# Wider rows of the token tile and wider weight-part buffers: the distance between the two operands of TensorE takes all multiples of 64 bytes

## The chip, the cores and the metric

One core of a Trainium2 chip runs the whole kernel. The metric is the device time of one execution in microseconds (us). TensorE (PE) multiplies, VectorE (DVE) and ScalarE (ACT) prepare operands and take results out of PSUM, GpSimd (POOL) fills a few tiles, and SyncE (SP) issues the weight transfers.

## What is computed

One layer of a diffusion backbone on 256 latent tokens and 256 context tokens, width D = 2048, all in float32:

```python
hx = modulate(rms_norm(x, norm1_g), sh1, sc1)          # the context tokens likewise
q, zf, zb, v, g, sb, sc, sh, ga, gb = split(hx @ w_in) # context: only zf, zb, v
o = hgrn2(q, zf, zb, v)                                # two directions, 8 heads, chunked scan
y_a = norm(o) * a_norm_g * silu(g)
y_b = sb * short_conv(sc * sh)
x = x + g1 * ((sigmoid(ga) * (y_a @ w_pa) + sigmoid(gb) * (y_b @ w_pb)) @ w_o)
a, b = split(modulate(rms_norm(x, norm2_g), sh2, sc2) @ w_up)
x = x + g2 * ((silu(dwconv3x3(a)) * b) @ w_down)
out = rms_norm(x, final_g)
```

## The kernel before, in words

**Three products for one.** Every operand of the large products is kept in two parts of type float32r, a high part and a low part (what is left of the float32 value when the high part is taken off). A product of tokens and weights is then made of three matmuls: high by high, low weights by high tokens, and high weights by low tokens.

**The tiles that TensorE reads.** `H` (line 175) holds the tokens: 128 partitions, 16 rows `k` (one for each 128 of D), and in each row four stretches of 256 elements: the latent tokens' low and high part (`hx = H[:, :, 0:2, :]`, line 176) and the context's high and low part. One row is 4 x 256 x 4 bytes = 4096 bytes. A piece of weights (128 x 2048 elements, 1 MB) comes by one SP transfer into one of four `raw` buffers (`wload`, line 70). `wsplit` (line 97) makes of each half a high part with ACT (line 118, buffer `w_hi`, five of 4096 bytes) and a low part with DVE (line 119). The low part goes to a `w_lo` buffer (five of 4096 bytes, on the right side of the memory behind the small unused tile `edge`), or, once the context's tokens are no longer needed, into the context's half of two rows of `H` (`context_parts`, `lo_ring`).

**Two shapes of matmul.** `proj` (line 399) makes 256 columns of a projection: for eight rows `k` and two halves `n` of 128 columns, a *wide* matmul (high weights loaded, `src[:, k]` moving: 512 elements, low and high tokens side by side), and then a *narrow* one (low weights loaded, `src[:, k, 1, :]` moving: 256 elements). Sixteen wide and sixteen narrow ones alternate, `wide_next` lets groups of one shape join up to 32. `token_product` (line 804) works for `w_o` and `w_down` the other way round: parts of tokens are loaded (from `mg`, or from `hx` by `y_part`), and 512 columns of `w_hi` or of a low part move; the output is named `to`. `values` (`vacc`) does the same for v, and `mm3` (line 139) with `proj_xc` and the first stage (`acx`, `zacc`) takes latent and context tokens together.

Each matmul comes with a load of its 128 x 128 weights into the array, and the load for the next matmul runs while the present one streams its moving operand. So at any time TensorE reads two places of the memory: the present matmul's moving operand and the next one's weights. I call the *distance* of such a pair the address where those weights begin, less the address where the moving operand begins, in remainder by 512 bytes.

**Addresses before.** In the built program `H` begins at byte 76288 of each partition, the `w_hi` buffers at 55808 and every 4096 after, `y_a` at 182784, `mg` at 150016. All of these, all row and buffer steps, and all slices that the products take (512, 1024 or 2048 bytes long) are multiples of 512. The `w_lo` buffers begin at 208832, which is 448 above a multiple of 512. So every pair of the products named above has the distance 0, but for those with a `w_lo` buffer: 448 where it is loaded, 64 where it moves.

**The rest that the change touches.** `cst` (line 164, `silu(c)` and `silu(c_ctx)` in 32 columns) is the weights operand of the first stage's products, and column 0 is also the scalar of line 691, where DVE sums the rows of `w_mod` for later segments. `pb` (line 162) holds the columns of `b_mod`. `squares` (line 856) writes a square that nobody reads, for the sum that comes with it. The order of the instructions on the engines is fixed when the program is built, in part by hand (`manual_schedule`, `issue_after`).

Of the kernel before, what the change touches and what calls it, by code (L numbers as in the profile page):

```python
# [9 lines left out]
F32 = mybir.dt.float32  # L10
F32R = mybir.dt.float32r
U8 = mybir.dt.uint8
AF = mybir.ActivationFunctionType
ALU = mybir.AluOpType
PSUM = bass.MemoryType.PSUM

P = 128
T = 256
D = 2048
KD = D // P  # L20
# [5 lines left out]
HB = 64  # L26
EPS = 1e-6
SPLIT = 2.0 ** 63


def strided(ap, offset, dims):
# [5 lines left out]
def hybrid_layer_kernel(ctx: ExitStack, tc: tile.TileContext, I, out, dbg=None):  # L37
    nc = tc.nc
# [3 lines left out]
    ctx_d = I["ctx"][0]  # L42
# [5 lines left out]
    cp = ctx.enter_context(tc.tile_pool(name="cp", bufs=1))  # L48
    rawp = ctx.enter_context(tc.tile_pool(name="rawp", bufs=4))
    hip = ctx.enter_context(tc.tile_pool(name="hip", bufs=5))  # L50
    hp = ctx.enter_context(tc.tile_pool(name="hp", bufs=1))
# [3 lines left out]
    lop = lop_cm.__enter__()  # L55
# [14 lines left out]
    def wload(parts):  # L70
        raw = rawp.tile([P, 2048], F32, name="raw", tag="raw")
        off = 0
        for src, shape in parts:
            n = 1
            for s in shape:
                n *= s
            dst = raw[:, off:off + n]
            if len(shape) == 2:
                dst = dst.rearrange("p (a b) -> p a b", a=shape[0])
            loads[0] = nc.sync.dma_start(dst, src)  # L80
            off += n
        return raw
# [4 lines left out]
    def lo_half():  # L87
        lo_ring.append(lo_ring.pop(0))
        return lo_ring[-1]

    def context_parts(*which):
        return [H[:, 2 * i:2 * i + 2, 2:4, :].rearrange("p a b t -> p a (b t)") for i in which]

# [3 lines left out]
    def wsplit(parts, widths=(1024, 1024), raw=None):  # L97


        if raw is None:  # L100
            raw = wload(parts)
        for i, n in enumerate(widths):
            half = raw[:, 1024 * i:1024 * i + n]
            hi = hip.tile([P, 1024], F32R, name="w_hi", tag="w_hi")[:, :n]
            if lo_ring:
                two = lambda ap: ap.rearrange("p (a n) -> p a n", a=2)
                lo = lo_half()
                operands = {"out": lo, "in0": two(half), "in1": two(hi.bitcast(F32))}
                cut = lambda a, b, lo=lo: lo[:, a // 512, a % 512:a % 512 + b - a]
            else:  # L110
                lo = lop.tile([P, 1024], F32R, name="w_lo", tag="w_lo")[:, :n]
                operands = {"out": lo, "in0": half, "in1": hi.bitcast(F32)}
                cut = lambda a, b, lo=lo: lo[:, a:b]
            with ExitStack() as behind:
                after, sub = behind_of.pop(0) if behind_of else ((), nc.vector)
                for ins in after:
                    behind.enter_context(tc.issue_after(ins.ins))
                nc.scalar.activation(hi, half, AF.Copy)  # L118
                sub.tensor_tensor(op=ALU.subtract, **operands)  # L119
            yield lambda p, a, b, hi=hi, cut=cut: cut(a, b) if p else hi[:, a:b]  # L120

    def wviews(parts, kt):

        n = 2048 // kt
        for i, part in enumerate(wsplit(parts)):
            for k in range(kt // 2):
                yield i * (kt // 2) + k, part(0, k * n, k * n + n), part(1, k * n, k * n + n)
# [8 lines left out]
    def mm(o, lhsT, rhs, start, stop):  # L136
        return nc.tensor.matmul(o, lhsT, rhs, start=start, stop=stop, skip_group_check=True)  # L137

    def mm3(o, wl, wh, k, start, stop):


        mm(o, wh, H[:, k, 1:3, :], start, False)
        mm(o, wl, H[:, k, 1:3, :], False, False)
        mm(o, wh, H[:, k, 0:4:3, :], False, stop)

# [13 lines left out]
    masks = cp.tile([P, 6, HB], U8)  # L159

    pa = cp.tile([P, 121], F32)
    pb = cp.tile([P, 96], F32)
    pf = cp.tile([P, 440], F32)
    cst = cp.tile([P, KD, 32], F32)
    lb = cp.tile([P, 16], F32)
    oml = cp.tile([P, 16], F32)
    bm = cp.tile([P, 2, 16], F32)
# [4 lines left out]

    H = hp.tile([P, KD, 4, T], F32R)
    hx = H[:, :, 0:2, :]


    first = ExitStack()
    sp = first.enter_context(tc.tile_pool(name="sp", bufs=1))  # L180
# [9 lines left out]
    for t in range(2):  # L190
        xt = xtp.tile([P, D], F32, name="xt", tag="xt")
# [5 lines left out]
    for t in range(2):  # L197
        parts = []
        for j in range(2):
            xt = lop.tile([P, 1024], F32, name="ct", tag="w_lo")  # L200
            nc.sync.dma_start(xt[:], ctx_d[t * P:t * P + P, 1024 * j:1024 * j + 1024])
            parts.append(xt[:])
        xts.append(parts)
    at = 0
    for src in (
# [6 lines left out]
        n = src.shape[0]  # L212
# [4 lines left out]
    def to_cols(dst, src, n):  # L217
        pt = psH.tile([P, 512], F32, name="pt", tag="psh")
        nc.tensor.transpose(pt[:, :n], src, ident[:n, :n])
        nc.vector.tensor_copy(dst, pt[:, :n])  # L220

    nc.vector.memset(cst[:], 0.0)
    to_cols(pa[:, 0:32], rows_c[:], 32)
    sg_c = sp.tile([P, 32], F32)
    nc.scalar.activation(sg_c[:], pa[:, 0:32], AF.Sigmoid)
    for i in range(2):
        nc.vector.tensor_tensor(out=cst[:, :, i], in0=pa[:, 16 * i:16 * i + 16], in1=sg_c[:, 16 * i:16 * i + 16], op=ALU.mult)

    ssq = sp.tile([P, 2, 4], F32)
    rstd = sp.tile([P, 4], F32)  # L230
    junk = H[:, 0].rearrange("p b c -> p (b c)")
    for i in range(2):
# [133 lines left out]
    with tc.manual_schedule(engines={nc.tensor.engine, nc.vector.engine, nc.scalar.engine}):  # L366
# [4 lines left out]
        for b, (k0, nk) in enumerate(blocks):  # L371
# [4 lines left out]
            if b + 1 < len(blocks):  # L376
                n = {0: (2, 8), 6: (5, 4), 7: (0, 3)}.get(b, (4, 6))
# [113 lines left out]
    def hgrn(g, ft, q):  # L491
# [10 lines left out]
        gc = gp.tile([P, 2, 2, T], F32, name="gc", tag="gc")  # L502
        nc.vector.tensor_scalar(out=X[:, 0:2], in0=ft[:, :, 0], scalar1=1.0 / SPLIT, scalar2=None, op0=ALU.max)
        nc.vector.tensor_scalar(out=gc[:], in0=ft[:, :, 1], scalar1=1.0 / SPLIT, scalar2=None, op0=ALU.max)
        nc.vector.tensor_scalar(out=ft[:], in0=ft[:], scalar1=SPLIT, scalar2=1.0, op0=ALU.mult, op1=ALU.min)
        nc.scalar.activation(X[:, 0:2], X[:, 0:2], AF.Ln)
# [174 lines left out]
    def mod_steps():  # L681
        for seg in (4, 3, 2, 5):
            acc = map_.tile([P, D], F32, name="macc", tag="macc")
            with ExitStack() as behind:
                if seg == 5:
                    behind.enter_context(tc.issue_after(h2_lo[KD // 2 - 1].ins))
                nc.gpsimd.memset(acc[:], 0.0)
            nc.gpsimd.dma_start(acc[0:1, :], b_mod[0:1, seg * D:seg * D + D])
            for k in range(KD):
                raw = wload([(w_mod[k * P:k * P + P, seg * D:seg * D + D], (2048,))])  # L690
                nc.vector.scalar_tensor_tensor(out=acc[:], in0=raw[:], scalar=cst[:, k, 0:1], in1=acc[:], op0=ALU.mult, op1=ALU.add)  # L691
                if k < KD - 1:
                    yield
            if seg in (3, 4):
                col = sh2 if seg == 3 else g2c
                for k4 in range(KD // 4):
                    pc = psH.tile([P, 4, P], F32, name="pc", tag="psh")
                    for k in range(4):
                        at = (4 * k4 + k) * P
                        nc.tensor.transpose(pc[:, k, :], acc[:, at:at + P], ident[:])  # L700
                    nc.vector.tensor_reduce(out=col[:, 4 * k4:4 * k4 + 4], in_=pc[:], op=ALU.add, axis=mybir.AxisListType.X)
                if seg == 4:
                    nc.vector.scalar_tensor_tensor(out=g2c[:], in0=g2c[:], scalar=1.0, in1=n2g, op0=ALU.add, op1=ALU.mult)
            else:
                yield
                for c, part in enumerate(wsplit(None, raw=acc)):
                    for n in range(2):
                        pm = psH.tile([P, 512], F32, name="pm2", tag="psh")
                        mm(pm[:], ones_r[:], part(0, n * 512, n * 512 + 512), True, False)
                        mm(pm[:], ones_r[:], part(1, n * 512, n * 512 + 512), False, True)  # L710
                        nc.scalar.copy(acc[:, c * 1024 + n * 512:c * 1024 + n * 512 + 512], pm[:])
                bcast[seg] = acc
            yield

    mods = mod_steps()

    def pump(n):
# [81 lines left out]
    tw = tw_cm.__enter__()  # L799
# [54 lines left out]
        nc.vector.tensor_tensor(out=x1[:, t, xs], in0=x1[:, t, xs], in1=tt[:, :n], op=ALU.add)  # L854

    def squares(dst, t, c0, n, pool):
        sq = pool.tile([P, 512], F32, name="sq", tag="sq", bufs=1)
        nc.scalar.activation(sq[:, :n], x1[:, t, c0:c0 + n], AF.Square, accum_out=dst)

    def root_of(t):  # L860
# [39 lines left out]
    for cq in range(4):  # L900
# [8 lines left out]
        for k2 in range(2):  # L909
            pt = psH.tile([P, 2, T], F32, name="ptx", tag="psh")  # L910
            for t in range(2):
                for i in range(2):
                    k = 4 * cq + 2 * k2 + i
                    nc.tensor.transpose(pt[:, i, t * P:t * P + P], x1[:, t, k * P:k * P + P], ident[:])
            with ExitStack() as behind:
                if cq == 3:
                    behind.enter_context(tc.issue_after(norm2.ins))
                for i in range(2):
                    k = 4 * cq + 2 * k2 + i
# [39 lines left out]
    tw = tw_cm.__enter__()  # L959
    w_up = I["w_up"][0]  # L960
    for j in range(NF // 2):
# [5 lines left out]
        for n in range(2):  # L967
# [4 lines left out]
            for dy in (0, -1, 1):  # L972
                for dx in (0, -1, 1):
                    if dy == 0 and dx == 0:
# [7 lines left out]
                                                   in1=c4[:, ro, co], op0=ALU.mult, op1=ALU.add)  # L982
# [25 lines left out]
    for cq in range(4):  # L1008
        accs = token_product(w_down, NF, cq, y_part, 2 if cq == 3 else 1)
        residual(accs, cq, bcast[5], td)  # L1010
        cs = slice(cq * 512, cq * 512 + 512)
# [3 lines left out]
    for t in range(2):  # L1015
        for cq in (0, 1, 3, 2):
            cs = slice(cq * 512, cq * 512 + 512)
# [40 lines left out]
```

## Time and profile before

| what | value |
|---|---|
| median of 3 runs | 1727.48 us (1726.83 to 1728.2) |
| the profiled execution | 1726.84 us |
| its span, first to last instruction | 1725.1 us |
| granted TensorE clock, mean | 0.996 |
| busy: PE / weight loads / DVE / ACT / POOL | 98% / 83% / 77% / 53% / 1% |
| moved by DMA | 384.84 MB, 223 GB/s |

PE and PEld are two rows of the same engine: matmuls, and the loads of their weights beside them. A matmul's span in the trace runs from its start to the end of its last result, so successive matmuls overlap in it; how fast they follow each other is read from their starts.

### The profile page before, as it was taken

How to read it: one execution, taken by the hardware profiler on the slowest of the kernel's cores; microseconds unless marked ns; L12 is line 12 of the kernel's file. 1: busy time of each engine (PE TensorE's matmuls, PEld its weight loads, DVE VectorE, ACT ScalarE, POOL GpSimd, SP SyncE). 2: the span in 40 equal slices, each digit the busy share in tenths (PEclk: the TensorE clock that was granted, in tenths of full speed). 3: DMA queues.
4: the chain of work that ended last, by engine and by line, in shares of the span. 5: the costliest groups of instructions: out<-in, count | busy, mean ns of one | idle time of the engine just before them, and what ended most of it. 6: DMA issues, size and time to landing. Idle time of an engine off the chain costs nothing.

```text
span 1725.1 us, 23733 instructions
## 1 busy us (share of the span) xinstructions
PE 1693.0 (98%) x9435; PEld 1425.7 (83%) x9435; DVE 1325.5 (77%) x1703; ACT 907.2 (53%) x1156; POOL 17.7 (1%) x24
## 2 busy tenths in 40 slices
PE   5999999999999999999999999999999999999998
PEld 3657888888888888888888788888888888888886
DVE  4336367668999889888875689988888887876774
ACT  5226346555755545445554555555545555665663
POOL 0000000000000010000000000000000000000000
PEclk9999999999999999999999999999999999999999
DMA  9996223233778779879876467777777755655552
GB/s 360 344 337 210 98 74 120 66 108 132 240 264 269 248 254 357 316 275 345 324 278 210 143 205 244 230 237 239 232 237 244 244 177 190 220 192 195 192 191 84
DMA packets 293045, 384.84 MB, mean 223 GB/s; under 512 B 7780, under 2 KB 245645, under 8 KB 284102
## 3 DMA queue, kind: packets, MB, share of 16 engines
q1 hardware_dynamic: 291824, 379.56, 64.6%
q10 hardware_dynamic: 838, 3.50, 0.5%
q8 instruction: 74, 1.21, 0.3%
q0 software_dynamic: 272, 0.26, 0.1%
q14 instruction: 37, 0.30, 0.0%
HBM read 381.20 MB, written 2.10 MB: 222 GB/s over the span
## 4 chain that ended last, share of the span: by engine, by line
PE 97%; ACT 1%; DVE 1%; issue 0%; DMA 0%; ACTq 0%; DVEq 0%
PE acc L137 57%; PE to L137 19%; PE acx L137 6%; PE vacc L137 5%; PE zacc L137 5%; PE pm L137 2%; PE ps L137 2%; PE po L137 1%; DMA rows_a<-in_norm_g_dram 0%; PE pt L249 0%; PE pm L326 0%; PE kdt L529 0%; PE pc L700 0%; ACT H L235 0%; DVE x L854 0%
## 5 line engine op out<-in xcount | busy, mean ns | idle before, releaser
L118 ACT ACTIVATE w_hi<-raw 128x1024 fp32r<-128x1024 f32 x506 | 532.6, 1058 | 418.1 <-PE acc L137 281.3
L137 PE MATMUL acc<-H,w_hi 128*128 128x512 f32 x2688 | 634.5, 391 | 2.3 <-DVE H L938 1.7
L119 DVE TENSOR_TENSOR H<-raw,w_hi 128x1024 fp32r<-128x1024 f32 x428 | 521.3, 1223 | 124.2 <-ACT w_hi L118 114.0
L137 PEld LDWEIGHTS acc<-H,w_hi 128*128 128x128 f32 x2688 | 498.6, 188 | 103.0 <-issue 1.8
L137 PEld LDWEIGHTS acc<-H 128*128 128x128 f32 x2360 | 295.2, 191 | 6.3
L137 PE MATMUL acc<-H 128*128 128x256 f32 x2360 | 300.3, 283 | 0.0
L137 PE MATMUL to<-w_hi,H 128*128 128x512 f32 (+1 forms) x712 | 217.1, 387 | 0.0
L691 DVE SCALAR_TENSOR_TENSOR macc<-raw,cst,macc 128x2048 f32<-128x2048 f32 x64 | 150.2, 2347 | 13.5 <-DMA raw<-in_w_mod_dram 12.3
L137 PEld LDWEIGHTS to<-w_hi,H 128*128 128x128 f32 x712 | 133.2, 188 | 27.1
L981 DVE SCALAR_TENSOR_TENSOR cvf<-av,pf,cvf 128x189 f32<-128x189 f32 (+2 forms) x352 | 134.7, 429 | 13.2 <-ACT cvf L969 12.7
L119 DVE TENSOR_TENSOR w_lo<-raw,w_hi 128x1024 fp32r<-128x1024 f32 x78 | 94.9, 1223 | 55.7 <-ACT w_hi L118 50.8
L137 PE MATMUL to<-H 128*128 128x512 f32 (+1 forms) x356 | 137.6, 387 | 0.0
L133 ACT ACTIVATE H<-y 128x512 fp32r<-128x512 f32 x88 | 55.2, 630 | 85.8 <-PE to L137 85.4
L137 PE MATMUL acx<-H,w_hi 128*128 128x512 f32 x288 | 93.4, 399 | 0.0
L134 DVE TENSOR_TENSOR H<-y,H 128x512 fp32r<-128x512 f32 x88 | 60.7, 692 | 36.2 <-ACT H L133 36.1
L137 PE MATMUL vacc<-w_hi,H 128*128 128x512 f32 x256 | 81.5, 394 | 0.0
L137 PE MATMUL zacc<-H,w_hi 128*128 128x512 f32 x224 | 78.1, 412 | 1.9 <-ACT H L337 1.9
L137 PE MATMUL to<-w_hi,mg 128*128 128x512 f32 (+1 forms) x264 | 79.9, 384 | 0.0
L137 PEld LDWEIGHTS to<-H 128*128 128x128 f32 x356 | 66.9, 188 | 13.7
L137 PEld LDWEIGHTS zacc<-H,w_hi 128*128 128x128 f32 x224 | 42.0, 190 | 26.3 <-issue 12.2
L137 PEld LDWEIGHTS acx<-H,w_hi 128*128 128x128 f32 x288 | 53.7, 188 | 12.1
L337 ACT ACTIVATE H<-xsT,md 128x256 fp32r<-128x256 f32 x32 | 16.8, 591 | 86.2 <-DVE md L331 86.2
(230 smaller groups left out, 1565.9 us busy)
## 6 DMA issues: line engine op xcount, KB each, us to landing
raw<-in_w_up_dram SPq DMA_DIRECT2D x88, 1024.0 KB, 4.9
raw<-in_w_in_dram SPq DMA_DIRECT2D x81, 1024.0 KB, 5.1
raw<-in_w_mod_dram SPq DMA_DIRECT2D x64, 1024.0 KB, 6.1
raw<-in_w_down_dram SPq DMA_DIRECT2D x44, 1024.0 KB, 5.0
raw<-in_w_mod_dram SPq DMA_DIRECT2D x64, 512.0 KB, 6.1
raw<-in_w_o_dram SPq DMA_DIRECT2D x16, 1024.0 KB, 5.2
raw<-in_w_in_dram SPq DMA_DIRECT2D x16, 512.0 KB, 3.8
raw<-in_w_pa_dram SPq DMA_DIRECT2D x8, 1024.0 KB, 6.1
```

What stands on the lines that cost most here:

```text
L118: nc.scalar.activation(hi, half, AF.Copy)
L119: sub.tensor_tensor(op=ALU.subtract, **operands)
L133: nc.scalar.activation(hi, src, AF.Copy)
L134: nc.vector.tensor_tensor(out=lo, in0=src, in1=hi.bitcast(F32), op=ALU.subtract)
L137: return nc.tensor.matmul(o, lhsT, rhs, start=start, stop=stop, skip_group_check=True)
L337: upper = nc.scalar.activation(H[:, kk, 1 + i, :], src, AF.Identity, scale=mv[:, 1, k, i:i + 1], bias=mv[:, 0, k, i:i + 1])
L691: nc.vector.scalar_tensor_tensor(out=acc[:], in0=raw[:], scalar=cst[:, k, 0:1], in1=acc[:], op0=ALU.mult, op1=ALU.add)
L981: nc.vector.scalar_tensor_tensor(out=c4[:, ro, co], in0=a4[:, ri, ci], scalar=pf[:, tap * NF + f:tap * NF + f + 1], in1=c4[:, ro, co], op0 ...
```

## The change

Rows of `H` and the buffers `w_hi`, `w_lo` (also where they hold the context's input) grow by `SHIFT` = 16 elements, 64 bytes. The room for it comes from `cst` and `pb`, which move into the pool `sp` that is given up after the first stage (a column of `cst` is copied to the small tile `cs` for line 691), and from the squares of the `w_o` stage, which now go to the latent half of the last row of `H` instead of a tile of their own.

```diff
+SHIFT = 16
...
-            hi = hip.tile([P, 1024], F32R, name="w_hi", tag="w_hi")[:, :n]
+            hi = hip.tile([P, 1024 + SHIFT], F32R, name="w_hi", tag="w_hi")[:, :n]
...
-                lo = lop.tile([P, 1024], F32R, name="w_lo", tag="w_lo")[:, :n]
+                lo = lop.tile([P, 1024 + SHIFT], F32R, name="w_lo", tag="w_lo")[:, :n]
...
-    pb = cp.tile([P, 96], F32)
     pf = cp.tile([P, 440], F32)
-    cst = cp.tile([P, KD, 32], F32)
+    cs = cp.tile([P, KD], F32)
...
-    H = hp.tile([P, KD, 4, T], F32R)
+    H = hp.tile([P, KD, 4 * T + SHIFT], F32R, name="H")[:, :, 0:4 * T].rearrange("p k (a t) -> p k a t", a=4)
...
-            xt = lop.tile([P, 1024], F32, name="ct", tag="w_lo")
-            nc.sync.dma_start(xt[:], ctx_d[t * P:t * P + P, 1024 * j:1024 * j + 1024])
-            parts.append(xt[:])
+            xt = lop.tile([P, 1024 + SHIFT], F32, name="ct", tag="w_lo")[:, 0:1024]
+            nc.sync.dma_start(xt, ctx_d[t * P:t * P + P, 1024 * j:1024 * j + 1024])
+            parts.append(xt)
...
+    pb = sp.tile([P, 96], F32)
+    cst = sp.tile([P, KD, 32], F32)
     nc.vector.memset(cst[:], 0.0)
...
+    nc.vector.tensor_copy(cs[:], cst[:, :, 0])
...
-                nc.vector.scalar_tensor_tensor(out=acc[:], in0=raw[:], scalar=cst[:, k, 0:1], in1=acc[:], op0=ALU.mult, op1=ALU.add)
+                nc.vector.scalar_tensor_tensor(out=acc[:], in0=raw[:], scalar=cs[:, k:k + 1], in1=acc[:], op0=ALU.mult, op1=ALU.add)
...
     def squares(dst, t, c0, n, pool):
-        sq = pool.tile([P, 512], F32, name="sq", tag="sq", bufs=1)
+        if pool is tw:
+            sq = hx[:, KD - 1].rearrange("p a t -> p (a t)")
+        else:
+            sq = pool.tile([P, 512], F32, name="sq", tag="sq", bufs=1)
```

In the built program `H` now begins at 74240 with rows 4160 bytes apart, `w_hi` at 53440 and `w_lo` at 208512 with buffers 4160 bytes apart. The pairs of the products then have each of the eight distances 0, 64, ..., 448, each about once in eight: as `k` goes up by one, the moving row goes up by 4160 bytes and the weights by 1024, so that the distance mostly changes after every second matmul. Of the narrow pairs with both operands in `H`, 288 of 2271 keep the distance 0. The engines' instructions stand in the same order as before, with the same waits on PE, ACT, DVE and SP; one DVE copy of 128 x 16 elements is added near the start.

## The prediction

> **What bounds the kernel now.** I read the page first (busy times and the chain), then the waits, then matmuls in order of time, in stretches where nothing is waited for.
>
> ```profile
> span 1725.1 us, 23733 instructions
> PE 1693.0 (98%) x9435; PEld 1425.7 (83%) x9435; DVE 1325.5 (77%) x1703; ACT 907.2 (53%) x1156; POOL 17.7 (1%) x24
> ...
> PEclk9999999999999999999999999999999999999999
> ```
>
> ```profile
> ACT w_hi L118 <- PE acc L137: 284.9, 238, 5.1
> ```
>
> TensorE is busy for 98% of the span at its full granted clock. Of the waits, ACT waiting for PE to free a buffer of weight parts is the longest: the makers of operands stand behind TensorE, not ahead of it. So the time is the number of matmuls times the interval at which they start, and only a change of that interval counts. Most matmuls are in these groups (count, busy us, mean ns of one):
>
> ```profile
> L137 PE MATMUL acc<-H,w_hi 128*128 128x512 f32 x2688 | 634.5, 391 | 2.3 <-DVE H L938 1.7 <-ACT ft L466 0.6
> L137 PE MATMUL acc<-H 128*128 128x256 f32 x2360 | 300.3, 283 | 0.0
> L137 PE MATMUL to<-w_hi,H 128*128 128x512 f32 x696 | 214.2, 389 | 0.0
> L137 PE MATMUL to<-H 128*128 128x512 f32 x348 | 135.4, 389 | 0.0
> L137 PE MATMUL to<-w_hi,mg 128*128 128x512 f32 x248 | 77.0, 391 | 0.0
> L137 PE MATMUL to<-H,mg 128*128 128x512 f32 x124 | 48.6, 392 | 0.0
> L137 PE MATMUL acc<-H,w_lo 128*128 128x256 f32 x328 | 43.8, 278 | 0.0
> L137 PE MATMUL acc<-y_a,w_hi 128*128 128x512 f32 x128 | 30.3, 389 | 0.0
> L137 PE MATMUL acc<-y_a,H 128*128 128x256 f32 x104 | 13.7, 283 | 0.0
> ```
>
> ```profile
> L137 PEld LDWEIGHTS acc<-H 128*128 128x128 f32 x2360 | 295.2, 191 | 6.3
> L137 PEld LDWEIGHTS acc<-H,w_lo 128*128 128x128 f32 x328 | 41.3, 188 | 0.9
> L137 PEld LDWEIGHTS acc<-y_a,H 128*128 128x128 f32 x104 | 13.5, 191 | 0.5
> ```
>
> This is the row pair on which everything rests. The same narrow matmul takes 283 ns, and its load 191, where the low weights lie in `H` (distance 0), and 278 and 188 where they lie in a `w_lo` buffer (448). Now the intervals, from starts in the timeline:
>
> ```profile
> 440.98 1.10 PE L137 MATMUL acc<-H,w_lo 128*128 128x256 f32 x8
> 441.92 2.08 PE L137 MATMUL acc<-H 128*128 128x256 f32 x16
> ...
> 453.04 1.07 PE L137 MATMUL acc<-H,w_lo 128*128 128x256 f32 x8
> 453.95 1.32 PE L137 MATMUL acc<-H,w_hi 128*128 128x512 f32 x5
> ...
> 999.71 3.34 PE L137 MATMUL acc<-H,w_hi 128*128 128x512 f32 x14
> 1002.88 1.11 PE L137 MATMUL acc<-H 128*128 128x256 f32 x8
> 1003.84 2.00 PE L137 MATMUL acc<-H,w_hi 128*128 128x512 f32 x8
> 1005.68 4.96 PE L137 MATMUL acc<-H 128*128 128x256 f32 x40
> 1010.47 1.78 PE L137 MATMUL acc<-H,w_hi 128*128 128x512 f32 x7
> ```
>
> Narrow at distance 0: (1010.47 - 1005.68) / 40 = 119.75 ns. Narrow at 448: (453.95 - 453.04) / 8 = 113.75 in one group and (441.92 - 440.98) / 8 = 117.5 in another, 115.6 in the mean. Wide at 0: (1002.88 - 999.71) / 14 = 226.4, but (1005.68 - 1003.84) / 8 = 230.0 in the first eight behind narrow ones. Where wide matmuls of mixed distances follow each other, two of three at 0 and one at 64 (`vacc`) or at 448 (`acx`), against `to` with 0 alone:
>
> ```profile
> 166.24 0.39 PE L137 MATMUL vacc<-w_lo,H 128*128 128x512 f32 x1
> ...
> 168.30 0.39 PE L137 MATMUL vacc<-w_lo,H 128*128 128x512 f32 x1
> ```
>
> ```profile
> 217.17 0.40 PE L137 MATMUL acx<-H,w_lo 128*128 128x512 f32 x1
> ...
> 218.56 0.39 PE L137 MATMUL acx<-H,w_lo 128*128 128x512 f32 x1
> ```
>
> ```profile
> 1500.20 0.61 PE L137 MATMUL to<-w_hi,H 128*128 128x512 f32 x2
> ...
> 1502.24 0.61 PE L137 MATMUL to<-w_hi,H 128*128 128x512 f32 x2
> ```
>
> Nine matmuls start from the first `vacc` row to the second: 2.06 / 9 = 228.9 ns. Six from one `acx` row to the other: 1.39 / 6 = 231.7. Nine in `to`: 2.04 / 9 = 226.7. My reading: the two reads can get into each other's way. Wide or narrow, every matmul has one load beside it, so among narrow ones loads come twice as often. Wide matmuls in an unchanging pattern settle after about eight where nothing is lost; narrow ones at distance 0 settle at 6 ns of loss. Patterns that change lose 2 to 5 ns in wide matmuls too. So the change has a good side and a bad one.
>
> **The change part by part.**
>
> *Narrow matmuls with weights in `H`*: 2360 + 104 = 2464. Seven of eight pairs leave the distance 0. For those I take 115.6, the mean of the two `w_lo` groups, since each of these is the same shape at another distance; for the eighth the old 119.75. Mean (7 x 115.6 + 119.75) / 8 = 116.1, gain 3.65 ns x 2464 = 9.0 us. Bounds: 113.75 everywhere gains 14.8, 117.5 everywhere 5.5, and 0 if distance isn't the cause.
>
> *Narrow matmuls with `w_lo`*: 328, from 115.6 to the same 116.1: 0.2 us lost, at most 0.6 either way (to 113.75 or 117.5).
>
> *Wide matmuls of `acc` and `to`*: 2688 + 128 = 2816 and 696 + 348 + 248 + 124 = 1416. They have the unchanging pattern today and lose it. Ends: 226.4 (nothing lost) and 231.7 (all like `acx`). I take 227.8, midway between `to` and `vacc`: `vacc` changes its distance as often as these will, but returns to 0, the bad one of the narrow rows, in two of three. `to`: 1.1 x 1416 = 1.6 us lost. `acc` today: of a group of 32, 8 at 230.0 and 24 at 226.4, mean 227.3; 0.5 x 2816 = 1.4 us lost.
>
> *Wide matmuls that have mixed distances already*:
>
> ```profile
> L137 PE MATMUL acx<-H,w_hi 128*128 128x512 f32 x288 | 93.4, 399 | 0.0
> L137 PE MATMUL vacc<-w_hi,H 128*128 128x512 f32 x256 | 81.5, 394 | 0.0
> L137 PE MATMUL zacc<-H,w_hi 128*128 128x512 f32 x224 | 78.1, 412 | 1.9 <-ACT H L337 1.9
> ```
>
> With a third matmul in `w_lo` for every two of these: 432, 384 and 336. From 228.9 (`vacc`) and 231.7 (the others) to 227.8: 0.4 + 3.0 = 3.4 us gained; none if they stay.
>
> *The other edits*: the copy to `cs` is one more small DVE operation, like this one:
>
> ```profile
> 11.36 0.25 DVE L220 COPY pa<-pt 128x89 f32<-128x89 f32 x1 [2.91 <-PE pt L219]
> ...
> 13.12 0.17 DVE L257 COPY bm<-pb 128x16 f32<-128x16 f32 x1
> ```
>
> It takes 0.17 us inside the 2.91 us that DVE waits ahead of the copy to `pa`: nothing, and 0.17 us if that wait were gone. The squares keep their size and place in ACT's queue and write to a row of `H` whose latent half was last read by the projections before `w_o`; nobody new waits. `cst` leaves its place long before other tiles take it. DVE and ACT read and write the same sizes at other addresses; with 23% and 47% of the span free, I cost that at nothing.
>
> Sum: -9.0 + 0.2 + 1.6 + 1.4 - 3.4 = -9.2 us. The profiled execution took 1726.84 us, 1.74 more than its span; the median shown is 0.64 above it. From the median: 1727.48 - 9.2 = 1718.3, say 1718.
>
> A rule speaks against all of it. The Trainium skill, "TensorE: Matmul & The Clock Gate", section "Step-by-step: what each phase is for", says that PE has two independent SBUF read ports, one for the moving operand and one for the weights, and that loading the next weights takes no read bandwidth from the running matmul. By that rule the sum would be 0 and the time 1727.5. The trace's 283 against 278 ns for the same shape does not agree with it.
>
> **The rivals.**
>
> *The wide matmuls lose more than the narrow ones gain (slower).* The place is `acc` and `to`, 4232 wide matmuls that run at 226.4 to 227.3 today just because the distance never changes. If ever-changing distances cost what `acx` shows, 231.7, they lose 4.4 x 2816 + 5.0 x 1416 = 19.5 us and `vacc` 2.8 x 384 = 1.1; the narrow ones, at 117.5, gain 5.5 less 0.6: 15.7 slower, 1743. It decides once the mean loss over 4232 passes what the narrow ones gain: with 9 us, 2.1 ns, about 229.2. For it: all three rows in which something changes (228.9, 230.0, 231.7). Against: all of them contain distance 0 mostly. Chance 0.25, with the halfway cases around 1733.
>
> *Distance is not what matters (no change).* The narrow rows differ by something else about `w_lo`, such as that weights and moving operand lie in different tiles; then 1727.5. Against: `acc<-y_a,H` has them in different tiles, at distance 0, and takes 283 and 191 like `acc<-H`. The Trainium skill's rule above would give the same time. Gains and losses that cancel belong here too. Chance 0.18.
>
> *Everything goes to the floor.* Narrow at 113.75, wide at 226.4: 14.8 + 0.6 + 0.9 x 2816 (2.5) + 0.3 x 1416 (0.4) + 2.5 x 384 (1.0) + 5.3 x 768 (4.1) = 23.4 us, 1704. Chance 0.11.
>
> **How the numbers follow.** My forecast has 0.46, its own range 1709 to 1724. About 0.2% (3.5 us) is what a measurement of this kernel can tell from no change. Faster: 0.46 + 0.11 = 0.57; same 0.18; slower 0.25. The range goes from 1706, which leaves out most of the floor case, to 1736, which takes in no change and the halfway cases of the slower rival and leaves out its full price.
>
> **What would show it.** In the profile after: narrow `acc<-H` from 283 to about 279 ns and its load from 191 to about 189, `to` from 389 to about 390, `acx` below 399. Narrow intervals still at 119.75 would refute the first term; wide ones at 230 or more in `acc` and `to` would show the slower rival. If TensorE's idle time grew, the bound would have moved, which I don't expect.

## The result and the profile after

The changed kernel takes 1742.74 us (median of 4 runs, 1740.4 to 1742.89) against 1727.77 us for the kernel before on the same chip: a ratio of 1.0084, 95% interval 1.0072 to 1.0097. It is 15 us slower, at the price of the slower rival (1743). Of all executions reported in this document one, of the run with low parts 192 bytes further on, took 3425.52 us; it is left out of that run's ratio.

The page after, to be held against the page of before: the span, the busy times, and the granted clock.

```profile
span 1741.0 us, 23734 instructions
...
PE 1708.5 (98%) x9435; PEld 1424.4 (82%) x9435; DVE 1327.4 (76%) x1704; ACT 907.2 (52%) x1156; POOL 17.6 (1%) x24
...
PEclk9999999999999999999999999999999999999999
```

The span grew by 15.9 us (1725.1 before) and PE's busy time by 15.5 (1693.0 before); DVE and ACT work as long as they did. The bound is where it was. The longest wait is ACT's for a buffer of weight parts, still on the far side of TensorE:

```profile
ACT w_hi L119 <- PE acc L138: 286.9, 235, 5.0
```

The matmuls by group (count, busy us, mean ns of one):

```profile
L138 PE MATMUL acc<-H,w_hi 128*128 128x512 f32 x2688 | 644.9, 395 | 2.3 <-DVE H L944 1.7 <-ACT ft L469 0.6
L138 PE MATMUL acc<-H 128*128 128x256 f32 x2360 | 296.8, 281 | 0.0
L138 PE MATMUL to<-w_hi,H 128*128 128x512 f32 x696 | 217.2, 393 | 0.0
L138 PE MATMUL to<-H 128*128 128x512 f32 x348 | 136.9, 393 | 0.0
L138 PE MATMUL acx<-H,w_hi 128*128 128x512 f32 x288 | 93.7, 400 | 0.0
L138 PE MATMUL acc<-H,w_lo 128*128 128x256 f32 x328 | 44.8, 282 | 0.0
...
L138 PEld LDWEIGHTS acc<-H 128*128 128x128 f32 x2360 | 291.9, 188 | 6.8
```

The narrow ones went from 283 to 281 ns and their loads from 191 to 188; the forecast had about 279 and 189. The wide ones rose, `acc` from 391 to 395 and `to` from 389 to 393, and `w_lo` went from 278 to 282. A mean of one matmul contains its pipeline, so the price is read from the starts. First `acc`, then `to`:

```profile
1014.33 4.90 PE L138 MATMUL acc<-H 128*128 128x256 f32 x40
1019.07 7.58 PE L138 MATMUL acc<-H,w_hi 128*128 128x512 f32 x32
1026.48 3.95 PE L138 MATMUL acc<-H 128*128 128x256 f32 x32
```

```profile
1499.64 0.62 PE L138 MATMUL to<-w_hi,H 128*128 128x512 f32 x2
...
1501.72 0.61 PE L138 MATMUL to<-w_hi,H 128*128 128x512 f32 x2
```

Narrow: (1019.07 - 1014.33) / 40 = 118.5 ns, where 40 at distance 0 took 119.75 each. Wide in `acc`: (1026.48 - 1019.07) / 32 = 231.6, where a settled group had 226.4. Nine of `to`: 2.08 / 9 = 231.1, where it was 226.7.

From here on, "mean interval" is the mean over all matmuls of a group in the trace, from the start of one to the start of the next, without those beside a stall. For narrow matmuls the weights named are the next matmul's, which are loaded meanwhile. Over the whole kernel:

| group (matmuls) | before | after | in all |
|---|---|---|---|
| narrow, weights in `H` (2462) | 119.60 | 118.21 | -3.4 us |
| narrow, weights in `w_lo` (335) | 115.75 | 118.45 | +0.9 us |
| wide, `acc` (2766) | 227.82 | 231.26 | +9.5 us |
| wide, `to` (1402) | 226.87 | 231.13 | +6.0 us |
| wide, `vacc` and `acx` | 229.15, 230.94 | 231.60, 232.18 | +1.4 us |

That is 14.4 of the 15.9 us. Another 1.4 lie in one place, the start of `w_up`. There TensorE waits 1.67 us in both kernels, and behind that wait the first wide matmuls start 426 or 427 ns apart, 5 of them before and 12 after. The granted clock is about half of full speed there (0.54 from 984.8 to 988.0 us before, 0.50 from 992.0 to 997.5 after). The first row is from the kernel before, the second from the one after:

```profile
984.90 1.62 PE L137 MATMUL acc<-H,w_hi 128*128 128x512 f32 x3 [1.67 <-DVE H L938]
...
992.11 8.19 PE L138 MATMUL acc<-H,w_hi 128*128 128x512 f32 x23 [1.67 <-DVE H L944]
```

The number of these intervals doesn't follow the distances: two of the runs below whose wide `acc` pairs are all as good as at distance 0 have 6 (the other edits alone) and 11 (constant 256). What sets it, no run shows.

The single intervals show how the wide ones got slower. A wide group in the kernel before, all at distance 0, and one after, with the distances in 64 bytes under it:

```
before  234 236 228 232 231 227 227 226 227 227 226 227 227 226 227 227 ...
after   232 232 240 235 225 230 233 233 234 235 231 226 229 230 232 227 ...
          6   6   5   5   4   4   3   1   0   0   7   7   6   6   5   0 ...
```

Before, the group is settled after five matmuls. After, it never is.

### The profile page after: what moved, and what is told of

The parts are those of the page before. It is cut to its first block, busy times and chain, and to the rows that moved or that the text cites. A ratio compares the mean times of both kernels' runs of the same rounds, so it can differ in the third digit from the quotient of the medians.

```text
span 1741.0 us, 23734 instructions
## 1 busy us (share of the span) xinstructions
PE 1708.5 (98%) x9435; PEld 1424.4 (82%) x9435; DVE 1327.4 (76%) x1704; ACT 907.2 (52%) x1156; POOL 17.6 (1%) x24
## 4 chain that ended last, share of the span: by engine, by line
PE 97%; ACT 1%; DVE 1%; issue 0%; DMA 0%; ACTq 0%; DVEq 0%
PE acc L138 57%; PE to L138 19%; PE acx L138 6%; PE vacc L138 5%; PE zacc L138 5%; PE pm L138 2%; PE ps L138 2%; PE po L138 1%; DMA rows_a<-in_norm_g_dram 0%; PE pt L252 0%; PE pm L329 0%; PE pc L703 0%; PE kdt L532 0%; ACT H L238 0%; DVE x L857 0%
## 5 line engine op out<-in xcount | busy, mean ns | idle before, releaser
L138 PE MATMUL acc<-H,w_hi 128*128 128x512 f32 x2688 | 644.9, 395 | 2.3 <-DVE H L944 1.7
L138 PE MATMUL acc<-H 128*128 128x256 f32 x2360 | 296.8, 281 | 0.0
L694 DVE SCALAR_TENSOR_TENSOR macc<-raw,cs,macc 128x2048 f32<-128x2048 f32 x64 | 150.1, 2346 | 13.4 <-DMA raw<-in_w_mod_dram 12.4
```

## The experiments

Two theories to begin with. **A**: the price lies in the change from matmul to matmul; where the distance stays the same, wide matmuls settle without loss. **B**: a distance other than 0 has a price of its own. The first question was which part of the change does it.

**The other edits alone** (no spreading; `w_lo` then lies at distance 256):

```diff
-SHIFT = 16
+SHIFT = 0
```

> The changed kernel with SHIFT = 0: rows of H and the w_hi and w_lo buffers are 4096 bytes apart again, all other edits stay (cst, pb, cs, squares into H). All distances are 0 again, but for w_lo (256 instead of 448). Theory A (a distance that changes from matmul to matmul costs the wide matmuls, the other edits cost nothing): about 1727.5 us, wide acc at about 391 ns in the group and to at 389. Rival (the other edits cost the 15 us): about 1742 us, with idle time on PE.

Measured: 1726.25 us, ratio 0.9998 (0.9988 to 1.0008). `cst`, `pb`, `cs` and the squares cost nothing, as forecast. One thing more: `w_lo` went from 448 to 256, and its narrow matmuls from 115.75 to 119.72, the value of distance 0. `acx` and `vacc`, which now mix 0 and 256 where they mixed 0 and 448 or 64, run at 227.96 and 227.22 instead of 230.94 and 229.15.

**Only the buffers apart** (rows of `H` stay at 4096):

```diff
-    H = hp.tile([P, KD, 4 * T + SHIFT], F32R, name="H")[:, :, 0:4 * T].rearrange("p k (a t) -> p k a t", a=4)
+    H = hp.tile([P, KD, 4 * T], F32R, name="H")[:, :, 0:4 * T].rearrange("p k (a t) -> p k a t", a=4)
```

> Only the w_hi and w_lo buffers are 4160 bytes apart, rows of H stay at 4096. Narrow pairs inside H keep the distance 0 (119.75 ns). The distance of the wide pairs of acc is one of 192 to 448 and holds for the eight matmuls of a buffer; in to, pairs with w_hi and with H alternate between two distances. Theory A (changing costs, any constant distance settles): acc wide partly settled, about 229 ns, so 2816 x 1.7 = 5 us lost, and to at 229 to 231, 3 to 6 us lost: 1735 to 1739 us. Rival B (each distance other than 0 has its own price in wide matmuls, constant or not): acc wide at 231.3 throughout, 1746 us.

Measured: 1744.44 us, 1.0101 (1.0086 to 1.0117), between the two forecasts and nearer to B. `acc` runs at 230.83, `to` at 232.17, and the narrow ones in `H`, back at 0, at 119.48. Eight wide matmuls of `acc` in a row come from one buffer here and keep their distance. They do settle, but not all to the same pace. The 32 intervals of one group, eight to a line with the mean of each line:

```profile
878.00 7.50 PE L138 MATMUL acc<-H,w_hi 128*128 128x512 f32 x32
```

```
226 229 232 226 229 231 226 229   228.5
232 226 229 232 226 229 231 227   229.0
227 226 227 227 226 227 227 226   226.6
235 231 236 231 236 231 235 230   233.1
```

**Only the rows of `H` apart**:

```diff
-            hi = hip.tile([P, 1024 + SHIFT], F32R, name="w_hi", tag="w_hi")[:, :n]
+            hi = hip.tile([P, 1024], F32R, name="w_hi", tag="w_hi")[:, :n]
...
-                lo = lop.tile([P, 1024 + SHIFT], F32R, name="w_lo", tag="w_lo")[:, :n]
+                lo = lop.tile([P, 1024], F32R, name="w_lo", tag="w_lo")[:, :n]
```

> Only the rows of H are 4160 bytes apart, the buffers stay at 4096. The distance of acc's wide pairs changes by 64 bytes with each row, after every second matmul, and that of narrow pairs too, nearly as in the changed kernel. Theory A: as the changed kernel, 1740 to 1743 us, wide at about 231 ns, narrow at about 118. Rival (the buffers' spacing is what costs): about 1727 or less.

Measured: 1742.55 us, 1.0092 (1.0077 to 1.0107); `acc` 230.94, `to` 231.86, narrow 118.48. That is where A put it, though B would have it slow as well. Each half of the change brings the whole loss, and the two don't add.

**One constant distance, 256.** `H` is laid out as two blocks, the latent rows one after the other and the context rows behind them, so that each row step is 2048 bytes; empty tiles between the pools set where the context block, `w_hi` and `w_lo` begin against the latent block:

```diff
-SHIFT = 16
+SHIFT = 0
+DIST = 64
+CTX = KD * 2 * T + DIST
...
+    pad1.tile([P, 64], F32, name="pad1")
...
-    H = hp.tile([P, KD, 4 * T + SHIFT], F32R, name="H")[:, :, 0:4 * T].rearrange("p k (a t) -> p k a t", a=4)
-    hx = H[:, :, 0:2, :]
+    H = hp.tile([P, CTX + KD * 2 * T], F32R, name="H")
+    hx = H[:, 0:KD * 2 * T].rearrange("p (k a t) -> p k a t", k=KD, a=2)
+    hc = H[:, CTX:CTX + KD * 2 * T].rearrange("p (k a t) -> p k a t", k=KD, a=2)
```

> Constant distance 256: the latent half and the context half of H are each one run of rows 2048 bytes apart, the context half, w_hi and w_lo begin 256 bytes off the latent half (in remainder by 512), y_a and mg lie as the latent half. Pairs of acc, to, acx, zacc have the distance 256 nearly throughout; those of vacc 0 and 256. Theory A (a constant distance settles without loss in wide matmuls; narrow ones at a distance other than 0 settle at 113.75 or 117.5): acc and to wide at 226.5, acx and zacc 4 to 5 ns faster, narrow at 115.6, so 1714 us, 1709 to 1720. Rival B (each distance other than 0 has its own price, constant or not): wide at about 231, narrow 118, 1740 us or more.

Measured: 1726.18 us, 0.9995 (0.9986 to 1.0005). Both missed. The timeline shows that 256 is simply 0 again:

```profile
1005.15 4.96 PE L146 MATMUL acc<-H 128*128 128x256 f32 x40
1009.94 7.44 PE L146 MATMUL acc<-H,w_hi 128*128 128x512 f32 x32
1017.22 4.00 PE L146 MATMUL acc<-H 128*128 128x256 f32 x32
```

Narrow (1009.94 - 1005.15) / 40 = 119.75, wide (1017.22 - 1009.94) / 32 = 227.5, in the mean 119.72 and 227.75. So the distance seems to count in remainder by 256, and of the eight distances of the change two, 0 and 256, are alike. That left two theories: **A2**, each distance in remainder by 256 has its own price for wide and for narrow matmuls; **C2**, only the change costs.

**Constant 64, 128 and 448.** The same kernel with other numbers (`DIST` in elements of 4 bytes: 16, 32, 112). `to` has the distance the other way round, since there the weight parts move: 448, 384 and 64.

```diff
-DIST = 64
+DIST = 16
```

> All operands keep one constant distance: 64 bytes in acc, acx, zacc and the narrow matmuls (64 mod 256), 448 (192 mod 256) in to. Theory A2 (distance 0 mod 256 is the one at which wide matmuls settle without loss; any other costs 2 to 5 ns in a wide matmul even when it never changes, and gains 2 to 5 ns in a narrow one): wide acc and to at 229 to 231, narrow at 115 to 118, time 1731 to 1742. Rival C2 (only the change from matmul to matmul costs; any constant distance settles): wide at 226.8 to 227.8 as before, narrow at 115.6, time about 1717.

> All operands keep one constant distance: 128 bytes everywhere, to too. Theory A2: wide at 229 to 231, narrow at 115 to 118, time 1731 to 1742. Rival C2 (only the change costs): wide 226.8 to 227.8, narrow 115.6, about 1717.

> All operands keep one constant distance: 448 bytes (192 mod 256) in acc, acx, zacc and the narrow matmuls, 64 in to. Theory A2: wide acc and to at 229 to 231; narrow at 115.75, as the low parts in w_lo had at this distance before; time 1731 to 1740. Rival C2 (only the change costs): wide 226.8 to 227.8, narrow 115.75, about 1717.

Measured: 1731.34 us, 1.0025 (1.0015 to 1.0036); 1749.85 us, 1.0137 (1.012 to 1.0154); 1732.74 us, 1.0037 (1.0024 to 1.005). C2 is out: none came near 1717. A2 holds in its mechanism. The runs with 64 and 448 are inside its ranges; 128 is 8 us above, because wide matmuls cost up to 233 ns where I had written 229 to 231. In `acc` at 64, 128 and 448, each from its own timeline:

```profile
1009.00 4.70 PE L146 MATMUL acc<-H 128*128 128x256 f32 x40
1013.54 7.62 PE L146 MATMUL acc<-H,w_hi 128*128 128x512 f32 x32
1021.00 3.79 PE L146 MATMUL acc<-H 128*128 128x256 f32 x32
```

```profile
1016.29 4.91 PE L146 MATMUL acc<-H 128*128 128x256 f32 x40
1021.03 7.63 PE L146 MATMUL acc<-H,w_hi 128*128 128x512 f32 x32
1028.50 1.70 PE L146 MATMUL acc<-H 128*128 128x256 f32 x13
```

```profile
1007.85 4.87 PE L146 MATMUL acc<-H 128*128 128x256 f32 x40
1012.56 7.50 PE L146 MATMUL acc<-H,w_hi 128*128 128x512 f32 x32
1019.89 3.93 PE L146 MATMUL acc<-H 128*128 128x256 f32 x32
```

Wide: 7.46 / 32 = 233.1 at 64, 7.47 / 32 = 233.4 at 128, 7.33 / 32 = 229.1 at 448. Narrow: 4.54 / 40 = 113.5, 4.74 / 40 = 118.5, 4.71 / 40 = 117.75. At 64 the narrow matmuls run at the floor of the prediction and the wide ones 6.7 ns above theirs. The mean intervals, with the cycles that the single ones repeat:

| distance, in remainder by 256 | wide `acc` | wide `to` | a wide cycle | narrow in `H` | narrow cycles |
|---|---|---|---|---|---|
| 0 | 227.75 | 226.80 | 226, 227, 227 | 119.72 | 120 |
| 64 | 232.96 | 233.32 | 236, 231 | 113.97 | 113, 114, 113 |
| 128 | 232.99 | 232.37 | 229, 238 | 118.55 | 115 to 123 |
| 192 | 229.04 | 228.93 | 226, 229, 232 | 116.11 | 113, 114, 113 or 118, 117, 118 |

The row of 0 is the run with 256. The `to` of row 64 is from the run with 448, that of row 192 from the run with 64. Wide and narrow matmuls want different distances, and 0 is the best of the four for the wide ones. The four lines of the run with only the buffers apart show the cycles of 192, 192, 0 and 64. Its five buffers lie at 192, 256, 320, 384 and 448; the mean of their prices for `acc` is 230.4, and 230.83 was measured. With that table, the spread in the changed kernel can be priced. The mean over the four rows is 230.7 for `acc`, 230.4 for `to` and 117.1 for the narrow ones; measured 231.26, 231.13 and 118.21. For the wide ones, 230.7 - 227.8 = 2.9 of the 3.4 ns lost in `acc`, and 3.5 of the 4.3 in `to`, belong to the distances themselves; by this reckoning, which takes the four as equally frequent, the rest goes to their changing.

**Two distances in one kernel.** High parts of the weights at 0, the context block with the low parts at 64, to give each shape its best row (against the run with constant 64):

```diff
-    pad1.tile([P, 112], F32, name="pad1")
+    pad1.tile([P, 128], F32, name="pad1")
...
-    edge.tile([P, 8], F32, name="edge")
+    edge.tile([P, 56], F32, name="edge")
```

> The high parts of the weights lie at distance 0 to the latent half of the tokens, and the low parts (in the context half of H) at 64 to it, so that wide matmuls in acc keep 0 and narrow ones keep 64. Theory A2 (each distance mod 256 has its own price by width: narrow 114.0 at 64 against 119.7 at 0, wide 227.75 at 0 against 233.0 at 64): narrow 2464 x -5.6 ns = -13.8 us, the 335 with w_lo -0.4, acc wide unchanged, to with one pair in three at 192 and two at 0 up to 228 or 228.5, +2; time 1712 to 1718, faster than before. Rival C3 (any change of distance from matmul to matmul undoes the settling): to at 231, +6, acc wide behind narrow ones at 229, +4; 1723 to 1727.

Measured: 1731.92 us, 1.0029 (1.0018 to 1.0039): both theories missed, on different terms.

```profile
1007.97 4.88 PE L146 MATMUL acc<-H 128*128 128x256 f32 x40
1012.68 7.44 PE L146 MATMUL acc<-H,w_hi 128*128 128x512 f32 x32
1019.96 3.93 PE L146 MATMUL acc<-H 128*128 128x256 f32 x32
```

Wide `acc` is at 7.28 / 32 = 227.5, as A2 said: narrow groups at 64 between them don't spoil it. But narrow is 4.71 / 40 = 117.75 here, not 113.5. The same distance has two stable cycles, and what ran before a group chooses: of 2367 narrow intervals followed by a narrow matmul with weights in `H`, 2071 were 113 or 114 ns in the run with constant 64, behind wide matmuls at 64; here, behind wide ones at 0, 2213 were 117 to 119. And `to`, where two pairs at 0 and one at 192 take turns, has 231.99, though either alone has 226.80 or 228.93. Their mean would be 227.5, so there the changing itself costs about 4.5 ns.

**Everything 64 bytes further on**: the layout in two blocks with all distances 0, and each tile 64 bytes up (the other empty tiles follow):

```diff
-    pad.tile([P, 64], F32, name="pad0")
+    pad.tile([P, 80], F32, name="pad0")
```

> Every operand, tokens and weight parts alike, starts 64 bytes further on than in the kernel with constant distances 0, so all distances stay 0. Theory A2 (only the distance between the two operands counts): narrow 119.7, acc wide 227.75, to 226.8, time 1726. Rival D (an operand's own place mod 256 counts, and the shifted rows were slow for that): wide at 229 to 233, time 1731 to 1745.

Measured: 1726.59 us, 0.9998 (0.9988 to 1.0007); narrow 119.71, `acc` 227.75, `to` 226.91. At distance 0, then, the place of the two operands together doesn't matter; at other distances and for other shifts this was not run.

**Low parts moved for narrow matmuls only.** Distance 0 everywhere, and the low parts 192 bytes (48 elements) further on in `H` while narrow matmuls load them; `w_o` and `w_down` get them at 0 again. `H` is 64 elements longer for it, and `y_b`, in its context block, begins 64 elements later (128 in the third run):

```diff
-            lo_ring += context_parts(0, 1, 2, 3)
+            lo_ring += context_parts(0, 1, 2, 3, off=48)
...
     w_up = I["w_up"][0]
+    lo_ring[:] = context_parts(*range(KD // 2), off=48)
...
     w_down = I["w_down"][0]
+    lo_ring[:] = context_parts(*range(KD // 2))
```

The second run has `off=16` (64 bytes), the third `off=112` (448 bytes).

> Distances 0 (mod 256) everywhere, as in the runs with constant 0 and 256, but low weight parts that narrow matmuls use lie 192 bytes further on in H (2,374 of 2,464 narrow pairs in H at 192 mod 256); those of to lie at 0. Theory A3 (a price for each distance and width, and a narrow group at a distance other than 0 ends in one of two cycles, 113.3 or 117.7, by the state in which it is entered; behind wide matmuls at 0 and with low parts at 448, that is 192 mod 256, the groups before were mostly in the first, mean 115.75): narrow 114.5 to 116 against 119.7, 9 to 12 us gained on 1726, wide and to unchanged; time 1714 to 1718. Rival C3 (any change of distance undoes the settling): acc wide behind narrow ones at 230 or more, narrow at 117.7; 1726 or above.

> As the run before it, with 64 bytes in place of 192. Theory A3: behind wide matmuls at 0 a narrow group at 64 falls into the slower cycle (117.7, as with the mixed distances), so 2 ns x 2374 = 4.8 us gained; 1720 to 1723. Rival (the price belongs to the distance alone, 114.0 at 64 as with constant 64): 1712 to 1714.

> As the run with low parts 192 bytes further on, with 448 (192 + 256), in the same order of instructions. If the prices repeat every 256 bytes (as constant 0 and 256 were alike): narrow 117.4 as at 192, time 1723.5 to 1725. If 448 is a distance of its own (low parts in w_lo lay at 448 in the kernel before, and most of their groups ran at 113.3): narrow 114.5 to 116, time 1716 to 1720.

Measured: 1724.07 us, 0.9981 (0.9972 to 0.9991); 1723.77 us, 0.9981 (0.9972 to 0.999); 1724.54 us, 0.9983 (0.9974 to 0.9992). All three beat the kernel before by about 3 us, and the changed one by over 18. The forecast for 64 (1720 to 1723) was missed by 0.8 us, that for 448 with prices that repeat (1723.5 to 1725) was met. The run with 64:

```profile
1008.86 7.44 PE L146 MATMUL acc<-H,w_hi 128*128 128x512 f32 x32
1016.14 3.93 PE L146 MATMUL acc<-H 128*128 128x256 f32 x32
1019.91 7.44 PE L146 MATMUL acc<-H,w_hi 128*128 128x512 f32 x32
```

Wide 7.28 / 32 = 227.5, narrow 3.77 / 32 = 117.8; `to` keeps 226.82. My 9 to 12 us for 192 were wrong: of 2372 narrow intervals followed by a narrow matmul with weights in `H`, 2097 were 117 to 119 ns and only 222 were 113 or 114, where 168 of 335 with `w_lo` in the kernel before had been 113 or 114. 448 gave the same means as 192 (117.38 narrow, 228.04 and 228.05 wide): the prices repeat every 256 bytes at these distances too.

The times show less than the narrow matmuls gain. In the run with 64 those with the next weights in `H` went from 119.60 to 117.59, which is 5 us, but those with `w_lo`, now at 256, lost 1.3 of it, and the way back to 0 ahead of `w_down` made TensorE wait for DVE's low parts:

```profile
1474.13 0.19 PEld L146 LDWEIGHTS to<-H 128*128 128x128 f32 x1 [1.31 <-DVE H L128]
1474.13 0.50 PE L146 MATMUL to<-H 128*128 128x512 f32 x1 [0.99 <-DVE H L128]
```

The intervals beside that wait are 1.4 us longer in sum than in the kernel before, and those of the small groups (transposes and short products) 1.8 us.

## Why the prediction was wrong

**The bound was right.** TensorE's intervals set the time, and their change with the distance gives 14.4 of the 15.9 us; 1.4 more come from the longer stretch at half the clock. The other edits had no part in it (1726.25 us without the spreading).

**The step that failed** is the price of the wide matmuls: "I take 227.8, midway between `to` and `vacc`". Measured 231.26 and 231.13. `acc` lost 9.5 us, not 1.4, and `to` 6.0, not 1.6: 12.5 of the 25 us between forecast (9.2 faster) and result (15.9 slower). Behind it stands the sentence "wide matmuls in an unchanging pattern settle after about eight where nothing is lost": it was read from distance 0 alone, the only unchanging distance of wide matmuls that the trace held, and said of all. At 64, 128 and 192 an unchanging pattern settles too, but into cycles of 229 to 233 ns. The reason that I gave against the slower rival, that its rows "contain distance 0 mostly" and 0 is the bad one, had it the wrong way round: 0 is bad for narrow matmuls and the best for wide ones. The rival's point of decision, 229.2 in the mean, lies below every constant price but those at 0 and at 192. That the rival's own sum, 15.7 us, came out so near is partly luck: it had 19.5 us for `acc` and `to` where 15.5 were lost, and 5.5 for the narrow ones where 3.4 were gained.

**Narrow matmuls in `H`.** The mechanism was right, the size not: 3.4 us for 9.0. The 115.6 stood on one distance, 448, and on two groups of it; the four distances have 119.7, 114.0, 118.6 and 116.1, of which 256 shares the first with 0, and changing adds about 1 ns.

**Narrow with `w_lo`**: 0.9 us lost for 0.2, the same error. **Rows that had mixed distances already**: 1.4 us lost where 3.4 were to be gained. Their prices of before had come from mixing 0 with 448 or 64; the way out of that was a constant distance (227.96 and 227.22 with 0 and 256), not more of them.

**The rule of two ports.** The Trainium skill, "TensorE: Matmul & The Clock Gate", section "Step-by-step: what each phase is for", says that loading the next weights takes no read bandwidth from the running matmul. The runs don't agree with what the prediction drew from it, that distance would then change nothing: with these float32r products, the same instructions and the same data, the distance alone moves a wide interval from 226.8 to 232.4 (`to` at 0 and at 128).

**What stays open.** Why the pattern repeats every 256 bytes, and what the two reads share, no run shows. Nor did I find a layout in which narrow matmuls keep 113.3 while wide ones keep 226.7; by an estimate from the table and the cycle of 113, 114, 113, (119.72 - 113.3) x 2462 = 15.8 us lie there, of which the best run here has 5 in its narrow intervals and 3 in its time.

## What to carry to other kernels

An unchanging pattern that runs well shows the price of its own setting and of no other: before a change spreads work over settings that the trace doesn't hold, measure each of them held constant, for each shape apart. A spread cost about the mean of those prices here, and the changing came on top. Where one setting is bad for one shape and best for another, count the larger share of the time first, and move only the operands of the shape that gains.

## What the runs showed of the hardware

With float32r matmuls back to back, each with a load of 128x128 weights beside it, and at full granted clock (0.994 to 0.996 over the whole kernel), the address of the next weights less that of the moving operand, in remainder by 256 bytes, sets the interval at the four distances that were run: 226.8 to 233.3 ns for 512 columns, 113.3 to 120 for 256. Where the two lie together made no difference at distance 0 (all operands 64 bytes further on: 1726.59 us). Intervals fall into short repeating cycles, at some distances one of two, and which one depends on what ran before (narrow at 64: 113.3 or 117.7). Behind a wait of 1.67 us the granted clock was about 0.5 for 5 to 12 wide matmuls, and their intervals 427 ns.
